# Start addresses of the buffers that TensorE reads, in a one-core trunk layer

## The chip, the cores and the metric

The kernel runs on one core of one Trainium2 chip. The metric is the time of one execution on the device in microseconds (us), the median of three runs. The engines are named as the profile names them: PE is TensorE's matrix multiplication, PEld its weight load, DVE is VectorE, ACT is ScalarE, POOL is GpSimd, SP issues most of the DMAs.

## The reference

One layer on 1024 tokens of 1024 features in float32. Four branches (a gated spatial mixing, a gated linear recurrence, latent attention with 8 heads, gated linear attention) read one projection of the normed input; each is mapped back to 1024 columns, weighted by a sigmoid gate, and their sum passes one more projection. Then a gated feed-forward part with a short convolution over the tokens follows.

```
h = rms_norm(x, norm_mix_pre); proj = h @ w_in
o_a, o_b, o_c, o_d = gmlp(..), rglru(..), mla(..), gla(..)
mixed = sum_k sigmoid(gate_k) * (o_k @ w_branch_k) @ w_out
x = x + rms_norm(mixed, norm_mix_post)
h = rms_norm(x, norm_ffn_pre)
z = causal_dwconv(h @ ffn_w_up) ; a, b = split(z)
x = x + rms_norm((gelu(a) * b) @ ffn_w_down, norm_ffn_post)
```

## The kernel before

**Products.** Every float32 matrix is split into two float32r parts, a high one and a rest (`split()`, lines 83 to 85: a cast on ACT, then a subtraction on DVE), and a product is three passes, high by high, high by rest, rest by high. One instruction multiplies a stationary operand of 128 x 128 words (512 bytes of each partition) with a moving operand of up to 512 columns (2048 bytes of each partition); each has its own weight load. The projections by features (`fm()`, line 139) stream 512 tokens of the split input `hh`, `hl` or of a branch `o` past weights from the weight slots `wh`, `wl`. The projections by tokens (`tm()`, line 148) stream 256 to 512 weight columns past 128 tokens. The feed-forward part streams the tokens `q` past the weights `wh`, `wl` (`fmh()`, line 1105, 48 products for one of 44 tiles) and then the down weights `dh`, `dl` past the activations `gh`, `gl` (`down()`, line 1159, 24 products for one accumulated pair).

**Order.** The program is written stage by stage; a scheduler of the framework places instructions on each engine's queue by their dependences, some stretches are kept in the order written. A stage's weights pass a rotation of slots: two raw slots `wr` that SP's DMAs fill, three slots `wh`, three slots `wl`. `weights()` (line 98) cuts a matrix into loads of `step` row blocks; a load that finds all three slots of `wh` in use waits for TensorE to read the oldest for the last time.

**Where buffers begin.** The pools lie one behind the other in a partition, constants first, then the weight slots, small values and 26 pages of 4096 bytes; the buffers of the right side (`hh`, `hl`, later the attention's keys and values, later the tokens `q`) are laid out from the other end. A weight slot has 1056 words, 4224 bytes, so that each begins 128 bytes further past a multiple of 256 than the one before. In the built program the slots of `wh` begin at bytes 28448, 32672 and 36896, those of `wl` at 41120, 45344 and 49568: past a multiple of 256 that is 32, 160, 32 and 160, 32, 160. So a weight tile has either `wh` at 32 and `wl` at 160 (two of three tiles) or `wh` at 160 and `wl` at 32 (the third). All pages begin 1568 bytes past a multiple of 2048 (32 past one of 256), all buffers of the right side 2016 past one of 2048 (224 past one of 256). The identity of the transposes begins at 16512.

The lines that the change touches are the first pools, the size of a weight slot (line 25), and the step of the load of `wd` in `gla()` (line 371), where 8 row blocks of 264 columns were loaded as two times four.

Of the kernel before, what the change touches and what calls it, by code (L numbers as in the profile page):

```python
# [10 lines left out]
F32 = mybir.dt.float32  # L11
# [6 lines left out]
P = 128  # L18
# [5 lines left out]
NF = FFN // P  # L24
WSLOT = 1056

# columns of the packed per-partition parameters
C_LCW, C_LCB, C_LBA, C_LBI, C_LAM, C_GBG, C_QN, C_KVN = 0, 16, 20, 24, 28, 32, 34, 37
C_FCW, C_FCB, C_END = 39, 39 + 3 * 2 * NF, 39 + 4 * 2 * NF
# columns of the constants  # L30
K_ID, K_ROT, K_INV, K_QUART, K_HPI, K_SGN, K_END = 0, 128, 256, 257, 258, 259, 260
# [12 lines left out]
class Trunk:  # L44
    def __init__(self, ctx, tc, a, out, dump=None, stop=99):
        self.tc, self.nc, self.a, self.out = tc, tc.nc, a, out
        self.ctx = ctx
        self.n = 0
        self.fetched, self.bg = {}, deque()
        self.dump = dump or (lambda name, src: None)  # L50
        self.stop = stop
        mk = lambda name, bufs, **kw: ctx.enter_context(tc.tile_pool(name=name, bufs=bufs, **kw))
        self.cp = mk("const", 1)
        self.wp = mk("weights", 3)
        self.sp = mk("small", 16)
        self.pp = mk("pages", 26)
        self.keep = self.cp
        self.mk = mk

# [1 line left out]
    def nm(self, base):  # L61
# [19 lines left out]

# [1 line left out]
    def split(self, src, hi, lo):  # L83
# [14 lines left out]
    def weights(self, src, K, n, step):  # L98
        """K row blocks of n columns, `step` blocks a load: k -> (hi, lo)."""
        out = []  # L100
        for k0 in range(0, K, step):
            kn = min(step, K - k0)
            hi, lo = self.weight(src[:, k0 * n:(k0 + kn) * n], kn, n)
            out += [(hi[:, j, :], lo[:, j, :]) for j in range(kn)]
        return out
# [3 lines left out]
    def pre(self, name, idx):  # L109
        """fetches a weight tile ahead of its use."""  # L110
        self.fetched[name, idx] = self.weights(self.a[name][idx], *self.SPEC[name])
# [6 lines left out]
    def tick(self, n=1):  # L118
        """issues n steps of the work that is not on the tensor engine's path."""
        for _ in range(n):  # L120
# [11 lines left out]
    def fm(self, ps, w, r, first=True, last=True):  # L132
        """ps[:, 1024 tokens] += w^T r for w = [(hi, lo)] and r = [(hi, lo)] over the row blocks."""
        K = len(w)
# [7 lines left out]
    def tm(self, ps, l, w, first=True, last=True):  # L142
        """ps[128 tokens, n] += l^T w for l = [(hi, lo)] and w = [(hi, lo)] over the row blocks."""
        K = len(w)
# [18 lines left out]

# [1 line left out]
    def consts(self):  # L165
# [12 lines left out]
    def norm_rows(self, x_i, gbc, hh, hl, i, hn=None):  # L178
        """rms norm of 128 tokens; then, in a second step, transposed to features by tokens and split."""
        nc = self.nc  # L180
# [7 lines left out]
        ps = self.psum()  # L188
# [19 lines left out]
    def pweights(self, src, K, n, step):  # L208
        """as weights(), held in pages."""
        nc, out = self.nc, []  # L210
# [101 lines left out]
    def lru(self, spatial):  # L312
        nc, a, prm = self.nc, self.a, self.prm
        # 4 * softplus(-lambda)
        lam = prm[:, C_LAM:C_LAM + 4]
# [30 lines left out]
        def chain(h, u, t, x, y):  # L346
            # with v = 4 softplus(-lambda) r: a = exp(-2 v), sqrt(1 - a a) = sqrt(tanh v) (1 + a)
            q = self.page("q")
# [31 lines left out]
    def gla(self):  # L380
# [3 lines left out]
        for c in range(2):  # L384
            w = self.weights(a["wd"][c], 8, 264, 4)
            for i in range(NT):
# [8 lines left out]
                self.tick()  # L395
        # gate rank by tokens, the unused rows are zero
        ps = self.psum()
# [22 lines left out]
        def logs():  # L420
            """log sigmoid of the gates, by features."""
            for p in range(2):
# [15 lines left out]
        def decays(p):  # L438
            """their sums over a chunk, from its start and to its end, as factors."""
            x, b, e2 = gx[p], gb[p], self.page("e2")  # L440
# [154 lines left out]
    def load_o(self, k, h, right=False, raw=None):  # L595
        """a branch's rows h, split."""
        if raw is None:
# [7 lines left out]
    def mixing(self, k, last=False):  # L605
        """acc += sigmoid(gate k) * (o_k w_branch_k)"""
        nc, a = self.nc, self.a
# [21 lines left out]
    def last_mixing(self, k):  # L629
        """the last branch on the stored sums, with its stored gates; the result is split."""  # L630
        nc = self.nc
# [30 lines left out]
    def rope_table(self):  # L662
        """rows: cos, -sin, sin of the 16 angles as the constants' sign and shift say, twice."""
        nc = self.nc
# [23 lines left out]
    def latent(self):  # L688
        """down projections of queries and keys, their norms, transposed and split."""
        nc, a, prm = self.nc, self.a, self.prm  # L690
# [19 lines left out]
        rk, rq = self.rsqrt(sk, 256, 8), self.rsqrt(sq, 384, 8)  # L710
        # rotary key: rows [0 | x1 x2 | x2 x1] by tokens
        stg = self.page("stg")
# [7 lines left out]
        outs = {C_KVN: [], C_QN: []}  # L720
        # the scores' scale rides on the queries
        gains = {C_KVN: prm[:, C_KVN:C_KVN + 2], C_QN: self.cp.tile([P, 3], F32, name="gq")}
# [26 lines left out]
    def attention(self, cq, ckv, stg):  # L749
# [3 lines left out]
        for h in range(2):  # L753
# [4 lines left out]
            cs.append(t)  # L758
        # rotary rows of the keys, the same for all heads
        kt = [[[rpage("kh"), rpage("kl")] for _ in range(2)] for _ in range(2)]  # L760
# [34 lines left out]
        def score(u, j):  # L795
            """the scores of 128 queries, their exponentials and the sums of these; yields after each product."""
            head, g = units[u]
# [14 lines left out]
            nc.vector.reduce_max(out=nb, in_=s, axis=AX.X, negate=True)  # L812
            # the short rows of a pair share a page
            if g < 2 and j:
# [18 lines left out]
        def flip(u, m):  # L833
            """two blocks of keys of the pair's rows, transposed and split; the last block has the second row only."""
            g = units[u][1]
# [14 lines left out]
        def weigh(u, m, ptt):  # L850
# [9 lines left out]
            if m < g:  # L860
                return
            # the upper rows hold the products of the values' first parts, the lower of their rests
            pr, rows = head // 2, slice((head % 2) * 64, (head % 2) * 64 + 64)
# [11 lines left out]

        # values by tokens
        wv = self.weights(a["uv"][0], 2, 512, 2)
# [31 lines left out]
        def load(h):  # L909
            """as load_o(), in smaller steps."""  # L910
            raw = self.page("oraw")
# [15 lines left out]
        class Fill:  # L927
            """work of the tensor engine that is spread over the steps."""

# [56 lines left out]
    def fm1(self, ps, w, r):  # L986
        """a half of the tokens; yields after each product."""
        K = len(w)
# [9 lines left out]
    def merge_out(self):  # L998
        """x2 = x + rms norm(mixed w_out), kept in DRAM, normed, transposed and split again.

        A tile of tokens passes its stages each a tile behind the one before; the rows lie where the pieces
        of the transposed halves come to lie."""
        nc, a = self.nc, self.a
# [10 lines left out]
        for n in range(2):  # L1014
            early = []
            if n == 0:
                # the last rows' sums come late
                early = [self.psum() for _ in range(4)]
# [80 lines left out]
    def fmh(self, ps, w, h):  # L1099
        """half h of the tokens of w^T h2."""  # L1100
        ps = ps[:, h * 512:(h + 1) * 512]
# [5 lines left out]
    def ffn(self, rest):  # L1107
# [3 lines left out]
        def first():  # L1111
            """the first tile's halves of the tokens apart, so that the last tokens' norm is covered."""
            pss = []
# [56 lines left out]
        def finish(fs, i):  # L1170
            """the last sums, normed, and the residual, in two steps."""
            ps, t, x_i = down(fs, i), acc[i], xs[i]
# [9 lines left out]
        def close(fs, i):  # L1182
            """as finish() for the last tile: the columns in halves, the gain before the norm is known."""
            t, x_i, junk = acc[i], xs[i], q[2][:, 1 + i % 3, :]
            ss = self.small(4)
            halves = (slice(0, 512), slice(512, 1024))
            for k, c in enumerate(halves):
                ps = down(fs, i, (c,))
                nc.vector.tensor_add(out=t[:, c], in0=ps[:, c], in1=t[:, c])  # L1189
                nc.scalar.activation(out=junk[:, c], in_=t[:, c], func=AF.Square, accum_out=ss[:, k:k + 1])  # L1190
                # the mean of squares so far
                add = ss[:, 2:3] if k else EPS
# [115 lines left out]
def tiles(w, n):  # L1308
    """[K, cols] -> [cols // n, 128, K // 128 * n]: each a contiguous load."""
    K, cols = w.shape  # L1310
    return np.ascontiguousarray(w.reshape(K // P, P, cols // n, n).transpose(2, 1, 0, 3)).reshape(cols // n, P, K // P * n)
# [52 lines left out]
```

## Time and profile before

| | |
|---|---|
| median of 3 runs | 2048.85 us (2048.62 to 2049.36) |
| span of the profiled execution | 2047.8 us |
| PE busy | 2014.1 us, 98% of the span |
| PEld busy | 1699.2 us, 83% |
| DVE, ACT, POOL busy | 949.5, 676.2, 160.3 us |
| DMA | 144.78 MB, mean 71 GB/s |

The profiled execution is known by its span, the time from its first to its last instruction; the median of the runs is 1.05 us over it, the time that lies around the span. A matmul's own duration in the trace (390 to 396 ns for 512 columns) overlaps the next one's, since products are pipelined. What a product costs is the distance from its start to the next one's start: the starts are in the timeline, and the chain of waits gives the sum of such distances for runs of equal products.

### The profile page before, as it was taken

To read this page: it belongs to the slowest core of one execution; us is meant where nothing else is said; L and a number is where in the kernel's file an instruction comes from. 1 tells how busy PE (TensorE), PEld (TensorE's weight loads), DVE (VectorE), ACT (ScalarE), POOL (GpSimd) and SP (SyncE) were. 2 spreads that over 40 slices of the span, in tenths; PEclk is the share of its full clock that TensorE was granted. 3 is DMA by queue.
4 is the path that set the end of the run, shared out by engine and by line. 5 is a ranking of instruction groups with operands and counts; after the bars stand their busy time and mean duration, and the time that the engine had idled before them with its cause. 6 is when DMAs were issued, how large, how long until landed. Compare 5 with 4: busy or idle time off the path is not lost. (4 is left out here: it accounts for less than half of the span.)

```text
span 2047.8 us, 24364 instructions
## 1 busy us (share of the span) xinstructions
PE 2014.1 (98%) x10284; PEld 1699.2 (83%) x10284; DVE 949.5 (46%) x1172; ACT 676.2 (33%) x971; POOL 160.3 (8%) x260
## 2 busy tenths in 40 slices
PE   8999999999999999999999999899999999999998
PEld 7888988988888888987788799788888888888886
DVE  5145444531262322132888753655454444444446
ACT  6216552321121211232777533332122222222222
POOL 2000100200000000011222102200000000000002
PEclk9999999999999999999999999999999999999999
DMA  5112212122221222122000542211111111111123
GB/s 198 32 52 72 95 42 67 58 68 96 69 77 57 67 77 79 58 73 72 13 26 31 196 167 96 93 62 52 42 52 42 62 33 61 42 52 42 52 78 128
DMA packets 43342, 144.78 MB, mean 71 GB/s; under 512 B 4880, under 2 KB 6560, under 8 KB 43232
## 3 DMA queue, kind: packets, MB, share of 16 engines
q1 hardware_dynamic: 35280, 114.90, 17.3%
q0 software_dynamic: 7808, 28.05, 3.7%
q8 instruction: 81, 1.33, 0.3%
q14 instruction: 29, 0.24, 0.0%
q10 hardware_dynamic: 144, 0.26, 0.0%
HBM read 118.03 MB, written 25.17 MB: 70 GB/s over the span
## 5 line engine op out<-in xcount | busy, mean ns | idle before, releaser
L1105 PE MATMUL ps<-q,wh 128*128 128x512 f32 x1408 | 440.8, 394 | 1.1 <-ACT q L84 1.1
L85 DVE TENSOR_TENSOR wl<-wr,wh 128x1024 fp32r<-128x1024 f32 (+5 forms) x157 | 165.1, 1053 | 486.0 <-ACT wh L84 475.2
L84 ACT CAST wh<-wr 128x1024 fp32r<-128x1024 f32 (+5 forms) x157 | 143.5, 914 | 590.3 <-PE ps L139 428.2
L1105 PEld LDWEIGHTS ps<-q,wh 128*128 128x128 f32 x1408 | 264.3, 188 | 63.3 <-ACT q L84 1.4
L1105 PE MATMUL ps<-q,wl 128*128 128x512 f32 x704 | 278.3, 395 | 0.0
L139 PE MATMUL ps<-hh,wl 128*128 128x512 f32 x768 | 241.9, 396 | 0.0
L139 PE MATMUL ps<-hl,wh 128*128 128x512 f32 x768 | 241.4, 395 | 0.0
L139 PE MATMUL ps<-hh,wh 128*128 128x512 f32 x768 | 240.9, 395 | 0.0
L1139 DVE SCALAR_TENSOR_TENSOR fy<-ps,prm,fy 128x1023 f32<-128x1023 f32 x88 | 112.8, 1282 | 257.9 <-ACT fy L1137 256.3
L139 PEld LDWEIGHTS ps<-hh,wl 128*128 128x128 f32 x768 | 144.3, 188 | 34.4
L139 PEld LDWEIGHTS ps<-hh,wh 128*128 128x128 f32 x768 | 143.3, 188 | 34.7 <-issue 0.5
L139 PEld LDWEIGHTS ps<-hl,wh 128*128 128x128 f32 x768 | 144.2, 188 | 33.4
L1105 PEld LDWEIGHTS ps<-q,wl 128*128 128x128 f32 x704 | 132.2, 188 | 31.6
L139 PE MATMUL ps<-o,wh 128*128 128x512 f32 x512 | 141.3, 395 | 0.5 <-DVE g L652 0.3
L1137 ACT ACTIVATE fy<-ps,prm 128x1024 f32<-128x1024 f32 x44 | 53.0, 1205 | 266.9 <-PE ps L1105 266.9
L1159 PE MATMUL ps<-dl,gh 128*128 128x512 f32 x352 | 137.4, 390 | 0.0
L1159 PE MATMUL ps<-dh,gl 128*128 128x512 f32 x352 | 137.1, 389 | 0.0
L1159 PE MATMUL ps<-dh,gh 128*128 128x512 f32 x352 | 136.8, 390 | 0.0
L139 PEld LDWEIGHTS ps<-o,wh 128*128 128x128 f32 x512 | 95.7, 188 | 23.8 <-PE ps L139 0.7
L148 PE MATMUL p<-wh,hh 128*128 128x264 f32 (+2 forms) x384 | 112.6, 294 | 0.0
L148 PE MATMUL p<-wl,hh 128*128 128x264 f32 (+2 forms) x384 | 112.5, 294 | 0.0
L148 PE MATMUL p<-wh,hl 128*128 128x264 f32 (+2 forms) x384 | 112.3, 293 | 0.0
(332 smaller groups left out, 3086.3 us busy)
## 6 DMA issues: line engine op xcount, KB each, us to landing
wr<-in_wf SPq DMA_DIRECT2D x48, 512.0 KB, 3.6
wr<-in_up SPq DMA_DIRECT2D x44, 512.0 KB, 3.5
wr<-in_down SPq DMA_DIRECT2D x22, 512.0 KB, 3.5
wr<-in_wb SPq DMA_DIRECT2D x32, 256.0 KB, 2.6
oraw<-spill POOLq DMA_DIRECT2D x15, 512.0 KB, 4.6
x<-in_x SPq DMA_DIRECT2D x8, 512.0 KB, 7.5
gate<-g POOLq DMA_DIRECT2D x8, 512.0 KB, 3.8
acc<-acc POOLq DMA_DIRECT2D x8, 512.0 KB, 3.5
```

What stands on the lines that cost most here:

```text
L84: self.nc.scalar.copy(out=hi, in_=src)
L85: self.nc.vector.tensor_sub(out=lo, in0=src, in1=hi.bitcast(F32))
L139: self.nc.tensor.matmul(ps[:, h * 512:(h + 1) * 512], lhs, rhs[:, h * 512:(h + 1) * 512], start=first and k == 0 and j == 0, stop=last and ...
L148: self.nc.tensor.matmul(ps, lhs, rhs, start=first and k == 0 and j == 0, stop=last and k == K - 1 and j == 2)
L1105: self.nc.tensor.matmul(ps, w[k][l], r[:, k, :], start=k == 0 and j == 0, stop=k == 7 and j == 2)
L1137: nc.scalar.activation(out=y, in_=ps, func=AF.Identity, scale=cw(2), bias=prm[:, C_FCB + idx:C_FCB + idx + 1])
L1139: nc.vector.scalar_tensor_tensor(out=y[:, s:S], in0=ps[:, 0:S - s], scalar=cw(2 - s), in1=y[:, s:S], op0=ALU.mult, op1=ALU.add)
L1159: nc.tensor.matmul(ps[:, c], l[:, tok], r[:, c], start=f == fs[0] and j == 0, stop=f == fs[-1] and j == 2)
```

## The change

The slots of the weights have 1024 words instead of 1056. The pool of small values moves ahead of the weights, a gap of 376 words is laid into the constants and one of 504 words at the right end. In the built program every weight slot, every page and every buffer of the right side then begins at a whole multiple of 2048 bytes. The constants are not moved to such a place: the identity begins at 18016, 1632 past a multiple of 2048. A load of `wd` with four row blocks of 264 columns would need 1056 words, so its step is three, and eight row blocks take three loads (3, 3 and 2) instead of two. What is computed stays as it was. The rest of the diff takes comments out; `LINE` is not used.

```diff
-WSLOT = 1056
+WSLOT = 1024
+GAP_LEFT, GAP_RIGHT = 376, 504
+LINE = 2048
...
         self.cp = mk("const", 1)
+        self.sp = mk("small", 16)
         self.wp = mk("weights", 3)
-        self.sp = mk("small", 16)
         self.pp = mk("pages", 26)
+
+        gap = ctx.enter_context(tc.tile_pool(name="gap", bufs=1, side="right"))
+        gap.tile([P, GAP_RIGHT], F32, name="gap_right")
+        self.cp.tile([P, GAP_LEFT], F32, name="gap_left")
...
-            w = self.weights(a["wd"][c], 8, 264, 4)
+            w = self.weights(a["wd"][c], 8, 264, 3)
```

The order of instructions moves in the stage of `wd` alone. There ACT casts the raw weights into `wh` between the copies of finished products. Around the change from the first half of `wd` to the second, ACT's queue holds before (the copies into `vd` are line 392 for the first half, line 394 for the second; the casts of 1056 words are `wd`, that of 1024 the next stage's first weight tile):

```order
L392 COPY vd_1741<-p_232_1917 128x248
L84 CAST wh_1978<-wr_1977 128x1056
L84 CAST wh_2215<-wr_2214 128x1024
L392 COPY vd_1741<-p_233_1944 128x248
L394 COPY vd_1738<-p_240_1983 128x264
```

and now (lines are numbered 6 higher):

```order
L398 COPY vd_1746<-p_235_1928 128x248
L90 CAST wh_1983<-wr_1982 128x792
L90 CAST wh_1989<-wr_1988 128x792
L398 COPY vd_1746<-p_236_1955 128x248
L90 CAST wh_1995<-wr_1994 128x528
L400 COPY vd_1743<-p_246_2000 128x264
```

All three casts of the second half now stand around the last copy of the first half, since the first half holds all three slots, and the next stage's first weight tile is no longer cast here. At the end of the second half ACT's queue holds before:

```order
L394 COPY vd_1741<-p_246_2139 128x264
L84 CAST wh_2221<-wr_2220 128x1024
L394 COPY vd_1741<-p_247_2165 128x264
L84 CAST wh_2298<-wr_2297 128x1024
L402 COPY gdt_2200<-ps_2191 16x1024
```

and now:

```order
L400 COPY vd_1746<-p_252_2156 128x264
L90 CAST wh_2232<-wr_2231 128x1024
L90 CAST wh_2238<-wr_2237 128x1024
L400 COPY vd_1746<-p_253_2182 128x264
L408 COPY gdt_2217<-ps_2208 16x1024
```

The next stage's first weight tile (`wh_2232`) has moved here, behind the last but one copy of the stage; two weight tiles are cast before the last copy instead of one.

## Rows read from the trace of the kernel before

**Rows 1.** The page: busy time of each engine, slices of PE and its granted clock.

```profile
PE 2014.1 (98%) x10284; PEld 1699.2 (83%) x10284; DVE 949.5 (46%) x1172; ACT 676.2 (33%) x971; POOL 160.3 (8%) x260
PE   8999999999999999999999999899999999999998
PEclk9999999999999999999999999999999999999999
```

**Rows 2.** Waits of PE, longest first: us in total, times, longest us.

```profile
PE ps L190 <- DVE hn L186: 7.8, 1, 7.8
PE ps L1069 <- DVE q L85: 3.5, 1, 3.5
```

**Rows 3.** The chain that ended last, in order: start us, us, what.

```profile
1368.27 11.13 PE ps L1105 x48
1379.40 5.47 PE ps L1159 x24
1384.87 11.13 PE ps L1105 x48
1396.01 5.47 PE ps L1159 x24
1401.48 11.21 PE ps L1105 x48
```

**Rows 4.** The page's groups of products: busy us, mean ns | idle before.

```profile
L1105 PE MATMUL ps<-q,wh 128*128 128x512 f32 x1408 | 440.8, 394 | 1.1 <-ACT q L84 1.1
L1105 PE MATMUL ps<-q,wl 128*128 128x512 f32 x704 | 278.3, 395 | 0.0
...
L1159 PE MATMUL ps<-dl,gh 128*128 128x512 f32 x352 | 137.4, 390 | 0.0
```

**Rows 5.** Single lines' busy time on PE: stretch, its us, busy (products).

```profile
484.00:823.00 339.00, 339.00 (x1460) 274.02 (x1460) 1.00 0.24 78
...
375.00:418.00 43.00, 43.00 (x369) 43.00 (x369) 1.00 0.20 68
```

**Rows 6.** Timeline of PE where L1159 follows L1105: start us, us, what.

```profile
1578.71 0.39 PE L1159 MATMUL ps<-dh,gh 128*128 128x512 f32 x1
...
1580.10 0.39 PE L1159 MATMUL ps<-dh,gh 128*128 128x512 f32 x1
...
1581.45 0.39 PE L1159 MATMUL ps<-dh,gh 128*128 128x512 f32 x1
...
1584.17 0.63 PE L1105 MATMUL ps<-q,wh 128*128 128x512 f32 x2
```

**Rows 7.** All engines' busy time in the attention's stretch.

```profile
884.00:1142.00 258.00, 251.89 (x1401) 210.40 (x1400) 178.55 (x402) 157.36 (x308) 56.99 (x68) 1.00 0.16 53
```

**Rows 8.** Timeline of PE where the latent projection changes its three weight loads.

```profile
853.34 0.31 PE L148 MATMUL p<-wh,hh 128*128 128x336 f32 x1
853.58 0.42 PE L148 MATMUL p<-wl,hh 128*128 128x336 f32 x1
853.84 0.32 PE L148 MATMUL p<-wh,hl 128*128 128x336 f32 x1
...
857.06 0.31 PE L148 MATMUL p<-wh,hl 128*128 128x336 f32 x1
857.39 0.57 PE L148 MATMUL p<-wh,hh 128*128 128x336 f32 x2
857.80 0.31 PE L148 MATMUL p<-wl,hh 128*128 128x336 f32 x1
```

**Rows 9.** Groups of 128 columns: a transpose by the identity, a product of two pages.

```profile
L843 PE MATMUL pp<-cst,prob 128*128 128x128 f32 x288 | 47.8, 276 | 1.0 <-POOL prob L831 0.2 <-DVE sm L827 0.2
...
L504 PE MATMUL ps<-qb,e 128*128 128x128 f32 x64 | 9.8, 276 | 0.0
```

**Rows 10.** Timeline of PE: a transpose of eight blocks among products by tokens.

```profile
30.98 0.28 PE L148 MATMUL p<-pwh,hl 128*128 128x256 f32 x1
31.10 1.04 PE L190 MATMUL ps<-cst,hn 128*128 128x128 f32 x8
```

## The prediction

> **What bounds the kernel now.** I read the busy times first: TensorE's products cover 2014.1 of 2047.8 us, 98%, in every slice of the span but the first and the last two or so, at a granted clock in the top tenth throughout, that is at the level of 2.4 GHz [rows 1]. Then the waits: the longest of PE's is 7.8 us at the start, the next 3.5 us [rows 2]. So no other engine decides, and no transfer does. The time is the number of products times the distance from one start to the next, and the question is whether an address can move that distance.
>
> For that I read the chain that ended last, because it runs through equal products and so gives exact sums of distances. A tile of the feed-forward part takes 11.13 us for 48 products, 11.13, then 11.21, and the pattern goes on like that, two short ones and a long one [rows 3]. Three is the number of weight slots. In a short tile 32 of the 48 weight loads read a slot of `wh` that begins 32 bytes past a multiple of 256, and 16 one of `wl` at 160; in the long one it is the other way round. With a and b for the two kinds of distance, 32a + 16b = 11.13 and 16a + 32b = 11.21, so a = 230.2 ns and b = 235.2 ns. The work beside these tiles is the same each time; that the place of the slots makes the 5 ns is my inference from the period. Then the down products, whose operands all begin 32 bytes past a multiple of 256: 5.47 us for 24, which is 227.9 ns [rows 3]. The timeline resolves them: the first six after a feed-forward tile take 1.39 us (231.7 ns each), while twelve later ones take 2.72 us, 226.7 ns each [rows 6]. Where all operands are of one class the pace settles; where classes alternate it does not.
>
> 512 columns at one a cycle of 2.4 GHz would be 213.3 ns. What lies above that is 19 ns in the feed-forward tiles (mean of two short ones and a long one: 33.47 us / 144 = 232.4 ns), 13 ns in the settled down products.
>
> **The change, part by part.** *Distances of products with 512 columns.* There are 2112 in line 1105 (1408 + 704) and 1056 in line 1159 (three groups of 352) [rows 4], 3120 in line 139 (48 projections of 48, 32 of a branch of 24 and eight of the recurrence of 6, by the loops), and 360 more in the attention's lines 807, 992 and 148, 6648 together. After the change all their operands are of one class, zero. No row of before shows an operand pair that begins at zero, so the price is bounded by the nearest rows: the settled 226.7 ns of the one pair that is of one class [rows 6], the 235.2 ns of the slots at 160, and, below, whatever is left above 213.3 ns. I take 226.7, from the row that is nearest in kind: one class for all streams.
>
> - Line 1105: 232.4 - 226.7 = 5.7 ns, times 2112 = 12.0 us.
> - Line 139: a stretch that holds nothing else has 1460 products in 339.00 us, 232.2 ns [rows 5]; 5.5 ns times 3120 = 17.2 us.
> - Line 1159: 227.9 - 226.7 = 1.2 ns, times 1056 = 1.3 us.
> - The attention's 360: 5.5 ns would be 2 us, but there PE is busy 251.9 of 258 us and waits for others now and then [rows 7]; I take 1 us.
>
> *Distances of products with 256 to 336 columns.* 2304 in line 148. A stretch of 256-column products gives 369 in 43.00 us, 116.5 ns, 10 ns over the 106.7 of a column a cycle [rows 5]. Their moving buffers start before at 32 past a multiple of 256, their stationary ones at 224; some run over a multiple of 2 KB and some don't. I take 0; 2 ns either way would be 5 us.
>
> *The load of `wd` in three pieces.* It adds two DMAs on SP, two casts on ACT, two subtractions on DVE, for the same words. Copies of finished products stand behind the casts on ACT, but TensorE has two buffers for these. What matters is that all three slots are held until the half ends. The latent projection does just that already, and its change of weights shows the price: distances of 0.24 and 0.26 us, then 0.33 and 0.41 us for two, where 0.15 is usual, so 0.09 + 0.11 + 0.18 + 0.11 = 0.5 us [rows 8]. `wd` has two such ends, between its halves and before the next stage's tile, whose cast has moved to the last but one copy. At the first the scheduler lets products of two token tiles alternate, at the second eight transposes lie ahead. I take 0.5 us for both; the bounds are 0 and 1.0.
>
> *The identity.* 520 transposes stream it, and it now runs over a multiple of 2 KB (1632 + 512 > 2048). Products of two pages, some of which do that today, have 276 ns each like the transposes [rows 9]. I take 0; 1 ns would be 0.5 us.
>
> *Everything else.* Addresses of DMA targets and of operands of DVE and ACT change too; these engines are at 46% and 33% [rows 1] and TensorE hides what they would lose.
>
> Sum: 12.0 + 17.2 + 1.3 + 1.0 - 0.5 = 31.0 us off the span of 2047.8, so 2016.8; with the 1.05 us by which the median stands above that span, **2018 us**. One nanosecond on all 6648 distances is 6.6 us, so this case alone reaches from 2008 to 2030.
>
> A rule stands against all of this. The row shows a tile of 48 products at 11.13 or 11.21 us by the weight slot it reads [rows 3]. The Trainium skill (TensorE: Matmul & The Clock Gate, Part 2, step 1) says that PE has two independent SBUF read ports and that "Loading the next tile's weights doesn't steal SBUF read bandwidth from the running matmul". By that rule the places of the weights would be worth nothing. The period of three in the trace doesn't agree with it.
>
> **The rivals.** *Below the settled pace.* The 13 ns that are left in the settled products may themselves come from the start 32 bytes past a line of memory, and vanish at zero. For: the excess over a column a cycle isn't a constant, 19, 13 and 10 ns in three places. A transpose of eight blocks lasts 1.04 us [rows 10], a single one 0.276 [rows 9], so its distance is 0.764 / 7 = 109 ns; if its 128 columns take two cycles each (106.7 ns), only 2.4 ns are left as a fixed cost, although each has its own weight load, and its moving operand, the identity, begins 128 past a multiple of 2048. Against: that is a slower stream, on which nothing may show. If all products fell to 2.4 ns of excess, the 512-column ones would have 215.7 ns: 16.7 x 2112 + 16.5 x 3120 + 12.2 x 1056 + 16 x 360 = 105 us, and those of line 148 some 8 ns x 2304 = 18 us; the end of this case is 2049 - 123 = 1926 us. It reaches from there to 2008; its middle is 1967.
>
> The Trainium skill (TensorE: Matmul & The Clock Gate, Back-to-back issue gap) gives N / 2.4 + 2.5 ns for a warm product, which is 215.8 ns for 512 columns and would put an estimate at this end; no row of before comes down to it.
>
> *Nothing.* The period of three could belong to something that goes with the slot and not with its address, such as which raw slot the DMA or the cast works on beside it. Then the distances stay, and 0 to 1 us for `wd` is all: 2049 us, within 2045 to 2053. The Trainium skill's rule on the two read ports would give this case too. Against: the down products have no such rotation and settle to a nanosecond [rows 6].
>
> *Slower.* Streams that start at the same place may meet each other at every line, weight load against moving operand. Then all products have the pace of the worst class, 235.2 ns: 2.8 x 2112 + 3.0 x 3120 + 7.3 x 1056 + 3 x 360 = 24 us, with `wd` and the identity 26: 2075 us. It decides as soon as the mean distance rises over (2112 x 232.4 + 3120 x 232.2 + 1056 x 227.9 + 360 x 232) / 6648 = 231.6 ns. Against: the best pair of before also starts its two streams at equal places.
>
> **How the numbers follow.** Settled pace 0.42; below it 0.28; nothing 0.13; slower 0.17. The likeliest gives 2018. For the range I leave out what of the second case lies below 1940 (its last 14 of 82 us, 0.05) and what of the slower case lies above 2062 (about half, 0.09). A measurement of this kernel can tell some 0.2%, 4 us, from no change. Faster by more than that: 0.42 + 0.28 + 0.01 = 0.71. Within: 0.12. Slower: 0.17.
>
> **What would show it.** In the chain of waits after the change, a tile of line 1105 and 48 products should take one and the same time, no period of three, 48 x 226.7 = 10.88 us; 24 of line 1159 should take 5.44. About 10.4 us would be the second case, 11.13 and 11.21 unchanged the third, 11.29 the slower one. Line 139's stretch should hold 1495 products in 339 us. Around the middle of `wd` no distance should stand out by more than 0.3 us. I am wrong if the tiles still have two times, if line 148's distances move by more than 2 ns, or if PE begins to wait elsewhere for DVE or ACT.

## The result

The changed kernel takes 2022.53 us (median of 4 runs, 2021.27 to 2024.03) against 2049.11 us of the kernel before on the same chip: a ratio of 0.9865, 95% interval 0.9851 to 0.9879. It is 1.35% faster, 26.6 us; 2018 was forecast.

The page of the changed kernel, in the columns of [rows 1], and below it its longest waits of PE, as [rows 2]:

```profile
span 2019.5 us, 24376 instructions
...
PE 1985.8 (98%) x10284; PEld 1700.7 (84%) x10284; DVE 949.9 (47%) x1174; ACT 677.3 (34%) x973; POOL 160.8 (8%) x260
...
PEclk9999999999999999999999999999999999999999
```

```profile
PE ps L196 <- DVE hn L192: 8.0, 1, 8.0
PE ps L1075 <- DVE q L91: 3.5, 1, 3.5
```

PE does as many products as before, at the same granted clock, and is busy for 28.3 us less; the span of the profiled execution is 28.3 us shorter. No wait of a microsecond or more came or went. The difference lies in the distance between products. The chain of waits (start us, us, what) shows it where [rows 3] showed 11.13, 11.13 and 11.21 us:

```profile
1351.59 10.88 PE ps L1111 x48
1362.47 5.44 PE ps L1165 x24
1367.91 10.88 PE ps L1111 x48
1378.79 5.44 PE ps L1165 x24
1384.23 10.88 PE ps L1111 x48
1395.11 5.44 PE ps L1165 x24
```

Both lines now have 226.7 ns per product, and every tile takes the same time. The projections by features follow (stretch, its us, PE busy and products; before it was 1460 in 339.00 us, [rows 5]):

```profile
484.00:805.00 321.00, 321.00 (x1418) 265.89 (x1417) 1.00 0.24 75
```

By this count that is 226.4 ns instead of 232.2. The count takes in a product that began before the stretch, so the quotient is a little small; from the first start in the stretch to the last one, a product takes 226.7 ns, and took 232.4 before. The products of 256 columns went the other way, by the count of such a stretch from 116.5 ns [rows 5] to 119.0, by their starts from 117.3 to 120.0:

```profile
375.00:410.00 35.00, 35.00 (x294) 35.00 (x293) 1.00 0.23 84
```

### The profile page after: what moved, and what is told of

Same layout as the page of the kernel before. It is cut to its first block, busy times and chain, and to the rows that moved or that the text cites. A ratio compares the mean times of both kernels' runs of the same rounds, so it can differ in the third digit from the quotient of the medians.

```text
span 2019.5 us, 24376 instructions
## 1 busy us (share of the span) xinstructions
PE 1985.8 (98%) x10284; PEld 1700.7 (84%) x10284; DVE 949.9 (47%) x1174; ACT 677.3 (34%) x973; POOL 160.8 (8%) x260
## 5 line engine op out<-in xcount | busy, mean ns | idle before, releaser
L1111 PE MATMUL ps<-q,wh 128*128 128x512 f32 x1408 | 433.5, 389 | 1.1 <-ACT q L90 1.1
L1111 PE MATMUL ps<-q,wl 128*128 128x512 f32 x704 | 273.7, 389 | 0.0
L145 PE MATMUL ps<-hl,wh 128*128 128x512 f32 x768 | 237.0, 389 | 0.0
L145 PE MATMUL ps<-hh,wl 128*128 128x512 f32 x768 | 236.5, 389 | 0.0
```

The source lines that it names most:

```text
L145: self.nc.tensor.matmul(ps[:, h * 512:(h + 1) * 512], lhs, rhs[:, h * 512:(h + 1) * 512], start=first and k == 0 and j == 0, stop=last and ...
L1111: self.nc.tensor.matmul(ps, w[k][l], r[:, k, :], start=k == 0 and j == 0, stop=k == 7 and j == 2)
```

## The experiments

Each kernel changes one thing against the kernel before or against the changed kernel; the last two change several. Places are bytes past a multiple of 256. A *difference* is the place of the stationary operand less that of the moving one, modulo 256; in the projections by features and the feed-forward tiles of 48 products the weights are the stationary operand, in the projections by tokens the tokens are. Three theories stood at the start: A, the two streams of a product must begin at one place modulo 256; B, only the alternation of the weight slots does harm; C, multiples of 2 KB count.

**The load of `wd` alone.** The kernel before with this edit, at its line 385:

```diff
-            w = self.weights(a["wd"][c], 8, 264, 4)
+            w = self.weights(a["wd"][c], 8, 264, 3)
```

> The kernel before with one edit, the load of wd in three pieces; all buffers stay where they were. Every theory expects the feed-forward tiles unchanged at 11.13, 11.13 and 11.21 us. My own term: 0 to 1.0 us longer, 0.5 us most likely.

2049.41 us against 2049.45, ratio 1.0000 (0.9991 to 1.0009). The three pieces cost nothing that can be measured in the time, and the period of three is there:

```profile
1402.27 11.13 PE ps L1105 x48
...
1418.87 11.13 PE ps L1105 x48
...
1435.48 11.21 PE ps L1105 x48
```

In the changed kernel the change of weights in the middle of `wd` does show two longer distances (timeline of PE: start us, us, what):

```profile
238.45 0.28 PE L154 MATMUL p<-wh,hh 128*128 128x264 f32 x1
238.76 0.39 PE L154 MATMUL p<-wl,hh 128*128 128x264 f32 x1
238.99 0.28 PE L154 MATMUL p<-wh,hl 128*128 128x264 f32 x1
239.11 0.28 PE L154 MATMUL p<-wh,hh 128*128 128x264 f32 x1
```

0.31 and 0.23 us where 0.12 is usual, 0.3 us over. The run with this edit alone shows the same two distances (0.29 and 0.23 us), the kernel before doesn't. Some 0.15 us more follow 3 us later in the changed kernel.

**Slots of 1024 words alone.** The kernel before with the edit above and

```diff
-WSLOT = 1056
+WSLOT = 1024
```

> The kernel before with weight slots of 1024 words (and wd in three pieces), no gaps: all weight slots begin 32 past a multiple of 256, pages 32, the right side still 224. Theory A (all streams of a product must begin at one place modulo 256): the feed-forward tiles lose their period of three but stay above 10.88 us, since weights are at 32 and tokens at 224; some 11.0 us, about 2035 us in all. Theory B (only the alternation of the slots disturbs): 10.88 us and 2023 us. Theory C (multiples of 2 KB count): no gain, 2049 us.

2051.79 us, ratio 1.0012 (1.0003 to 1.0021): no gain, if anything a loss. Its chain:

```profile
1402.08 11.20 PE ps L1105 x48
1413.28 5.46 PE ps L1159 x24
1418.74 11.20 PE ps L1105 x48
```

The period of three is gone, so it did belong to the slots' places. But all tiles now have the longer time, and theory B falls: nothing alternates and nothing is gained. Theory A had the direction but not the size, 11.0 us expected. In its terms weights at 32 meet tokens at 224, a difference of 64; the next runs say whether that is what costs.

**Multiples of 256, none of 2048.** The changed kernel with

```diff
-GAP_LEFT, GAP_RIGHT = 376, 504
+GAP_LEFT, GAP_RIGHT = 56, 56
```

> The changed kernel with smaller gaps: every weight slot, page and right buffer begins at a multiple of 256 bytes, none at one of 2 KB (768, 768 and 1792 past it). Theories A and B: as the changed kernel, tiles of 10.88 us, 2022 us. Theory C: back to the time before, 2049 us, or between.

2023.21 us, ratio 0.9872 (0.9858 to 0.9885), tiles of 10.88 us:

```profile
1401.36 10.88 PE ps L1111 x48
1412.24 5.44 PE ps L1165 x24
```

**All places at 32.** The changed kernel with the left gap taken out and a right gap of 48 words.

```diff
-GAP_LEFT, GAP_RIGHT = 376, 504
+GAP_LEFT, GAP_RIGHT = 0, 48
...
-        self.cp.tile([P, GAP_LEFT], F32, name="gap_left")
```

> The changed kernel with gaps such that all these buffers begin 32 bytes past a multiple of 256. Theories A and B: as the changed kernel, tiles of 10.88 us, 2022 us, since zero is nothing special. Theory C, and a theory that a start within a line of 64 bytes costs something: slower than the changed kernel by 1 ns or more per product, 2029 us or more.

2021.98 us, ratio 0.9868 (0.9854 to 0.9881), tiles of 10.88 us:

```profile
1401.30 10.88 PE ps L1110 x48
1412.18 5.44 PE ps L1164 x24
```

Both runs give the whole gain with no buffer at a multiple of 2 KB, the second with none at a multiple of 64 bytes. Theory C falls, and so does the thought that a start within a line costs something by itself. What all kernels with the gain have in common is equality: both streams of these products begin at one place modulo 256.

**Alternating slots, all else at 0.** The changed kernel with `WSLOT = 1056` and `GAP_LEFT = 56`.

> The changed kernel with slots of 1056 words again (wd stays in three pieces): weight slots alternate between 0 and 128 past a multiple of 256, pages and the right side stay at 0. Theory A (weights and moving operand of a product must begin at one place modulo 256): tiles of two times again, over 10.88 us, the one with 32 loads at 128 the longer; line 139 back over 230 ns; 2035 to 2050 us in all. Theory A2 (one place modulo 128 is enough): 10.88 us and 2023 us.

2050.46 us, ratio 1.0003 (0.9994 to 1.0013): the gain is gone. The chain:

```profile
1402.79 11.09 PE ps L1111 x48
1413.89 5.44 PE ps L1165 x24
1419.33 11.09 PE ps L1111 x48
1430.42 5.45 PE ps L1165 x24
1435.87 11.21 PE ps L1111 x48
```

The short tile has 32 products of equal places, on `wh`, and 16 with a difference of 128, on `wl`; they come as two of `wh`, one of `wl`. The timeline of PE and PEld shows that the weights of the next product are loaded while a product streams; the load of `wl` at 1403.55 runs beside the second of the two products of `wh`:

```profile
1403.09 0.40 PE L1111 MATMUL ps<-q,wl 128*128 128x512 f32 x1
1403.09 0.42 PEld L1111 LDWEIGHTS ps<-q,wh 128*128 128x128 f32 x2
1403.32 0.62 PE L1111 MATMUL ps<-q,wh 128*128 128x512 f32 x2
1403.55 0.19 PEld L1111 LDWEIGHTS ps<-q,wl 128*128 128x128 f32 x1
```

By the starts in the trace the first product of `wh` takes 227 ns, the second 233 and that of `wl` 234: 16 times their sum is 11.10 us, the short tile. So an equal product beside which unequal weights are loaded has lost the pace too. In the long tile `wl` is the equal one, no two equal products follow each other, and all 48 have some 233.5 ns (11.21 us).

**Slots and pages at 128, tokens at 0.** The changed kernel with `GAP_LEFT = 88`.

> The changed kernel with another left gap: all slots and pages at 128 past a multiple of 256, the right side at 0. Nothing alternates; weights and tokens differ by 128. Theory A: feed-forward tiles of one time, over 11.0 us, line 139's products with branch operands (pages) settled, those with the input not; line 1159 at 5.44 us; 2035 to 2055 us. Theory A2: as the changed kernel, 10.88 us, 2023 us.

2051.98 us, ratio 1.0008 (0.9998 to 1.0017). Nothing alternates, and the tiles take 11.19 us; a place modulo 128 is not enough:

```profile
1403.95 11.19 PE ps L1111 x48
1415.15 5.45 PE ps L1165 x24
```

**The right gap taken out.** The changed kernel with

```diff
-        gap = ctx.enter_context(tc.tile_pool(name="gap", bufs=1, side="right"))
-        gap.tile([P, GAP_RIGHT], F32, name="gap_right")
```

> The changed kernel without its right gap: slots and pages stay at multiples of 2 KB, the right side is back at 224 past a multiple of 256, so weights minus tokens is 32. Theory A: tiles of one time over 10.88 us, 11.0 to 11.2 us, 2030 to 2050 us: the small gap alone carries most of the gain. If only a difference of 64 bytes or more counts: 10.88 us, 2022 us.

2051.49 us, ratio 1.0013 (1.0004 to 1.0023). Weights and pages still begin at multiples of 2 KB; moving the tokens by 32 bytes takes back everything (theory A had 2050 us at most):

```profile
1401.17 11.20 PE ps L1109 x48
1412.37 5.47 PE ps L1163 x24
```

This run also holds a comparison within itself. Line 143 (line 139 of before) reads the same weight slots for the input `hh`, `hl`, which lies on the right side, and for the branches `o`, most of which lie in pages (timeline of PE):

```profile
492.90 0.63 PE L143 MATMUL ps<-hh,wh 128*128 128x512 f32 x2
...
499.90 1.09 PE L143 MATMUL ps<-o,wh 128*128 128x512 f32 x4
...
501.29 1.07 PE L143 MATMUL ps<-o,wh 128*128 128x512 f32 x4
...
505.37 0.63 PE L143 MATMUL ps<-hh,wh 128*128 128x512 f32 x2
```

The 30 products of the input take 7.00 us, 233.3 ns each, at a difference of 32. The first six of the branch, at a difference of 0, take 1.39 us, 231.7 ns each; the next 18 take 4.08 us, 226.7 ns each. The run with slots and pages at 128 shows the same in its trace, as theory A expected there: some 233 ns for the input, 227 for the branches once settled.

**Three more differences.** The changed kernel with slots and pages at 0 (`GAP_LEFT = 56`) and the right side at 64, 32 and 96 (`GAP_RIGHT` = 40, 48 and 32).

> The changed kernel with slots and pages at 0 and the right side at 64 past a multiple of 256, so weights minus tokens is 192. Theory A: tiles of one time over 11.0 us, about the 235 ns that before had at this difference, 11.3 us; 2045 to 2060 us. If the difference counts only modulo 64: 10.88 us, 2022 us.

> The changed kernel with slots and pages at 0 and the right side at 32 past a multiple of 256: weights minus tokens is 224. If only equality helps: tiles over 11.1 us, 2045 to 2055 us. If the pace of 512 columns falls steadily from a difference of 128 over 192 to 256: tiles of 10.9 to 11.0 us, 2025 to 2033 us.

> As the run before, with the right side at 96: weights minus tokens is 160. If only equality helps: tiles of 11.2 us. If the pace falls steadily from 128 to 256: about 11.1 us.

The first gives 2033.98 us, ratio 0.9920 (0.9903 to 0.9936), the second 2053.69, ratio 1.0018 (1.0008 to 1.0027), the third one run of 2052.70. Their tiles, in this order:

```profile
1391.18 11.00 PE ps L1111 x48
1402.18 5.49 PE ps L1165 x24
```

```profile
1401.47 11.20 PE ps L1111 x48
```

```profile
1402.07 11.21 PE ps L1111 x48
```

So a tile of 48 products takes 10.88 us at a difference of 0; 11.20 at 32; 11.20 at 64; 11.19 at 128; 11.21 at 160; 11.00 at 192; 11.20 at 224. Of these differences 0 alone gives the pace in full, and there is no steady fall towards it. 192 stands out: it gives more than half of the gain, where theory A expected none. Why is open.

**A difference of 16.** The kernel of the next paragraph, with loads of 128 columns laid 4 words into their slot and those of 256 columns at its start.

> The kernel of slots of 1088 words, with loads of 128 columns (lines 139 and 1105 of before) laid 16 bytes into the slot and all others at its start: weights minus tokens is 16 for these. If equality is needed to within less than 32 bytes: feed-forward tiles of 11.2 us, about 2050 us. If starts within one run of 32 bytes are alike: 10.88 us, 2022 us.

One run of 2037.98 us against 2051.31 before on the same chip. The feed-forward tiles keep their time, the projections by features don't (chain; then the stretch 490 to 700 us of line 146, the changed kernel's line 145):

```profile
1400.97 10.88 PE ps L1112 x48
1411.85 5.44 PE ps L1166 x24
```

```profile
490.00:700.00 210.00, 210.00 (x901) 170.05 (x900) 1.00 0.22 69
```

901 products in 210 us are 233 ns. Neither answer expected covers both. The two lines read the same slots at the same difference. They differ in the order of their products: line 1112 goes from one moving buffer to the other and back, line 146 streams the two halves of one buffer past weights that it loads twice. Whether that order is what decides at 16 bytes was not tested.

**A version for narrow products too.** In two of the runs above the output gates' products of 256 columns, whose moving operand is the weights, had 113 ns by their starts: at a difference of 192 with slots of 1024 words alone, at 64 with the right side at 64. They have 120 when equal. Here the second of these runs, in the stretch that holds 294 products in the changed kernel:

```profile
375.00:410.00 35.00, 35.00 (x312) 35.00 (x310) 1.00 0.24 84
```

So the slots got 1088 words (17 times 256 bytes, wide enough for `wd` in two pieces), and loads of 256 columns begin 16 words into a slot:

```diff
-WSLOT = 1024
-GAP_LEFT, GAP_RIGHT = 376, 504
+WSLOT = 1088
+GAP_LEFT, GAP_RIGHT = 56, 56
...
         w = kn * n
+        c = slice(16, 16 + w) if n == 256 else slice(0, w)
-        nc.sync.dma_start(out=raw[:, 0:w], in_=src)
-        self.split(raw[:, 0:w], hi[:, 0:w], lo[:, 0:w])
+        nc.sync.dma_start(out=raw[:, c], in_=src)
+        self.split(raw[:, c], hi[:, c], lo[:, c])
...
-            w = self.weights(a["wd"][c], 8, 264, 3)
+            w = self.weights(a["wd"][c], 8, 264, 4)
```

> The changed kernel with slots of 1088 words (4352 bytes, 17 times 256), so that wd fits in two pieces again and all slots still begin at one place modulo 256; loads with 256 columns are laid 64 bytes into the slot. If the difference between weights and moving operand modulo 256 is all that counts: feed-forward tiles stay at 10.88 us, and the 960 products of 256 columns that stream from the slots go from 120 ns to the 113 ns that a difference of 64 or 192 had in two runs, 6.4 us less than the changed kernel, 2016 us. If those 113 ns came from something else in those runs: 120 ns, 2022 us.

2019.14 us (median of 4), ratio to before 0.9854 (0.9837 to 0.9870); the span is 2016.4 us, 3.1 less than the changed kernel's. The two intervals overlap, so the times alone don't rank the two. The feed-forward tiles keep their time, though the slots are now 17 times 256 bytes apart, which is no multiple of 512; so a difference of a multiple of 256 counts as none:

```profile
1397.43 10.88 PE ps L1112 x48
```

The trace shows narrow products closer together (first the output gates, then the merge; below it the changed kernel's merge):

```profile
375.00:410.00 35.00, 35.00 (x300) 35.00 (x299) 1.00 0.23 83
...
1190.00:1230.00 40.00, 40.00 (x355) 40.00 (x354) 1.00 0.36 132
```

```profile
1190.00:1230.00 40.00, 40.00 (x336) 40.00 (x335) 1.00 0.34 125
```

By their starts in these stretches the merge's products fell from 120.0 to 113.4 ns as expected, the output gates' only to 117.8. Over the whole trace the 960 products gave 3.6 us of the expected 6.4. Why the gates, at the same difference of 192, kept a slower pace than in the earlier run with that difference is open.

## Why the prediction was right, point by point

The bound was read rightly. PE was and is 98% busy, and the time went where the distances went.

The terms, worked out by adding all distances from start to start of a line's products in both traces: line 1105 fell by 12.1 us (12.0 forecast), line 139 by 17.1 (17.2), line 1159 by 0.8 (1.3). The settled pace of 226.7 ns, taken from the one pair of operands that was of one class, is the pace that these lines now have where nothing else stands between their products. Tiles of 10.88 and 5.44 us were named, and stand in the chain.

Two terms were off; with what they measured the sum would be 27.7 us instead of 31.0, and the span fell by 28.3. The attention's products gave 0.2 us and not 1. Their places are equal too, but the middle one of their distances only went from 233 to 232 ns: some runs of them have 227, others scatter from 224 to 238 as before. Waits and products of other widths stand between them there; that these keep the pace from settling is likely and not shown. And line 148 was put at 0 with 2 ns as its bound: its products of 256 columns became slower by 1.8 us in sum, all of 148's forms of 256 to 336 columns by 2.5. That is 1.1 ns each, but the output gates moved by 2.7, over the 2 ns that the prediction named as a sign of being wrong. The row that was at hand (116.5 ns, by the starts 117.3) came from unequal places, and equality, best for 512 columns, is not best for 256.

The forecast of the median, 2018 us, missed by 4.5 us, more than that of the span. The 1.05 us that stand for the time around the span compare a median with the span of another execution: every run here for which both are listed takes 1.72 to 1.84 us more than its own span. And the profiled execution of the changed kernel is the fastest of its four, 1.26 us under their median.

`wd` was put at 0.5 us; alone it measured 0.0 +- 1.8 us, and the trace of the changed kernel shows 0.3 us at its middle and some 0.15 behind it, inside the bounds. The identity's move left nothing to see: the transposes of [rows 9] still have 276 ns.

One reason was wrong, though the number that hung on it was right. I put the slower pace down to classes that alternate. The run with slots of 1024 words has no alternation and 11.20 us; the one with the right gap taken out likewise. What mattered is a property that the down products also had, that the two streams begin at one place modulo 256; "all of one class" is that property only where weights and moving operand are counted together, as the sum did. The two distances of 230.2 and 235.2 ns, one for each place of the slots, were a wrong reading too. Alone, the first one's difference of 64 has 233.3 ns (11.20 us / 48), the second one's of 192 has 229.2 (11.00 / 48), the other way round; and the run with alternating slots shows that the distance of a product also hangs on the weights that are loaded beside it, so that a distance for each slot could not be had that way.

The rivals. *Below the settled pace* didn't happen: in no run do products of 512 columns come under 226.7 ns over a tile, at a place of 0, 32 or any other. By the Trainium skill (TensorE: Matmul & The Clock Gate, Back-to-back issue gap) a warm product of 512 columns would have N / 2.4 + 2.5 = 215.8 ns, an estimate from that formula; no run here shows it. *Nothing* was excluded by the result. By the Trainium skill (TensorE: Matmul & The Clock Gate, Part 2, step 1) loading weights takes no read bandwidth from the running product. The run with alternating slots doesn't fit a load that costs the product nothing, 227 or 233 ns by the place of the weights loaded beside it; whether read bandwidth is what the product loses, no run shows. *Slower* had it the wrong way round for 512 columns: not equal places cost, but unequal ones, 6 to 7 ns per product at most differences, and the kernel before had paid most of that. For 256 columns equal places are the slower ones, as that rival had them, by 2 to 7 ns against a difference of 64 or 192.

## What to carry to other kernels

Where TensorE is the bound and each product has its own weight load, look at the places of the two operands against each other, modulo 256 bytes: in this kernel 32 bytes decided over 1.3%. That holds for float32r products of 512 columns; narrow ones have to be measured by themselves. A slot size that is not a multiple of 256 bytes showed here as a period in the chain of waits with the length of the rotation. The multiple of 2 KB was more than was needed, and a slot that is a little larger (1088 words) kept the load in two pieces.

## What the runs showed that was not expected

- The pace of a product of 512 columns is 226.7 ns at equal places and 233 ns at differences of 32, 64, 128, 160 and 224; at 192 it is 229 (11.00 us / 48). At 16 it is 226.7 in one line and 233 in another.
- For 256 columns it is the other way round: 120 ns at equal places, 113 to 118 at a difference of 64 or 192, by the stretch.
- An equal product has 233 ns instead of 227 when unequal weights are loaded beside it (11.09 us for a tile with two thirds of equal products). Behind a stretch of unequal products the first six equal ones can still be slower (231.7 ns in the run without the right gap).
- What in the memory or in TensorE makes the difference count was not seen; the traces hold times only.
